# A half-rotary kernel: one DMA queue for loads and stores, six resident tiles, tables loaded by GpSimd, and whole-tile VectorE operations with the sin products in PSUM

## Chip, cores and metric

The kernel runs on one core of one Trainium2 chip. The metric is device time in microseconds (us), median over executions; the profile's "span" is 1.7 to 1.8 us shorter than the time, in runs 5 to 8 and 12 it is 1.9 to 2.2 us shorter, so differences of 0.3 us between groups of runs are not read here. All runs told of here were fast (granted clock 1.0).

The names: VectorE (DVE in the profile) does the arithmetic; SP, ACT (ScalarE) and GpSimd (POOL) here issue transfers. Each has its own DMA queue (q1 is SP's, q10 ACT's, q0 GpSimd's), and all queues feed the same 16 DMA engines. A queue that hands out its transfers in order is also called a ring. HBM is the chip's main memory; SBUF and PSUM are the core's own memories, 128 partitions each.

## The reference

`x` is 16 x 512 x 16 x 64 (batch, sequence, heads, dim) in float32, 33.55 MB; `cos` and `sin` are 512 x 32. Of each 64 elements the first 32 are rotated in two quarters of 16, and the last 32 pass through.

```python
x1, x2 = x[..., :32], x[..., 32:]
first  = x1[..., :16] * cos[..., :16] - x1[..., 16:] * sin[..., :16]
second = x1[..., :16] * sin[..., :16] + x1[..., 16:] * cos[..., :16]
return np.concatenate([first, second, x2], axis=-1)
```

All of `x` is read and all of the output is written: 67.1 MB through the core's DMA engines, with little arithmetic.

## The kernel before

A tile is 4 MB: 128 partitions with eight rows (32 KB, contiguous in HBM) each. There are T = 8 tiles. Loads go out on SP's queue, stores on ACT's; VectorE works on half tiles.

```python
K = 8; T = B * S // (P * K)                                       # T = 8 tiles
x_pool = ctx.enter_context(tc.tile_pool(name="xp", bufs=5))       # five resident tiles
ab_pool = ctx.enter_context(tc.tile_pool(name="abp", bufs=1))
stage = const_pool.tile([PB, 2, K, HF], fp32)
nc.scalar.dma_start(out=stage[:, 0]..., in_=cosf)                 # tables, ACT's queue
nc.scalar.dma_start(out=stage[:, 1]..., in_=sinf)
# ... table: four VectorE copies of stage ...
KC = 4
for t in range(T):
    x_t = x_pool.tile([P, K, H, D], fp32)
    nc.sync.dma_start(out=x_t..., in_=xf[t])                      # load, SP's queue
    for k0 in range(0, K, KC):                                    # two halves
        x1 = x_t[:, k0 : k0 + KC, :, 0:HF]
        # ... c, s: broadcast views of the table ...
        nc.vector.tensor_mul(out=a_t[:], in0=x1, in1=c)
        nc.vector.tensor_mul(out=b_t[:], in0=x1, in1=s)
        nc.vector.tensor_sub(out=x1[:, :, :, 0:Q], in0=a_t[:, :, :, 0:Q], in1=b_t[:, :, :, Q:HF])
        nc.vector.tensor_add(out=x1[:, :, :, Q:HF], in0=a_t[:, :, :, Q:HF], in1=b_t[:, :, :, 0:Q])
    nc.scalar.dma_start(out=of[t], in_=x_t...)                    # store, ACT's queue
```

Below, L0 to L7 are the loads and S0 to S7 the stores of the eight tiles.

Of the kernel before, what the change touches and what calls it, by code (L numbers as in the profile page):

```python
# [1 line left out]

# [4 lines left out]


@with_exitstack
def kernel(  # L10
    ctx: ExitStack,
    tc: tile.TileContext,
    x: bass.AP,
    cos: bass.AP,
    sin: bass.AP,
    out: bass.AP,
):
    nc = tc.nc
    fp32 = mybir.dt.float32
    P = 128  # L20
    B, S, H, D = x.shape
    Q = D // 4
    HF = D // 2


    K = 8
    T = B * S // (P * K)
    PB = S // K
    REP = P // PB

    xf = x.rearrange("b s h d -> (b s h d)").rearrange("(t p f) -> t p f", t=T, p=P)
    of = out.rearrange("b s h d -> (b s h d)").rearrange("(t p f) -> t p f", t=T, p=P)
    cosf = cos.rearrange("(p k) j -> p (k j)", k=K)
    sinf = sin.rearrange("(p k) j -> p (k j)", k=K)

    const_pool = ctx.enter_context(tc.tile_pool(name="const", bufs=1))
    x_pool = ctx.enter_context(tc.tile_pool(name="xp", bufs=5))
    ab_pool = ctx.enter_context(tc.tile_pool(name="abp", bufs=1))

    stage = const_pool.tile([PB, 2, K, HF], fp32)  # L40
    nc.scalar.dma_start(out=stage[:, 0].rearrange("p k j -> p (k j)"), in_=cosf)  # L41
    nc.scalar.dma_start(out=stage[:, 1].rearrange("p k j -> p (k j)"), in_=sinf)


    table = const_pool.tile([P, 2, K, 2, Q], fp32)
    for r in range(REP):
        for t in range(2):
            nc.vector.tensor_copy(  # L48
                out=table[r * PB : (r + 1) * PB, t],
                in_=stage[:, t, :, 0:Q].unsqueeze(2).to_broadcast((PB, K, 2, Q)),  # L50
            )
    C = table[:, 0].rearrange("p k c j -> p k (c j)")
    Sn = table[:, 1].rearrange("p k c j -> p k (c j)")

    KC = 4
    for t in range(T):
        x_t = x_pool.tile([P, K, H, D], fp32)
        nc.sync.dma_start(out=x_t.rearrange("p k h d -> p (k h d)"), in_=xf[t])  # L58
        for k0 in range(0, K, KC):
            x1 = x_t[:, k0 : k0 + KC, :, 0:HF]  # L60
            c = C[:, k0 : k0 + KC].unsqueeze(2).to_broadcast((P, KC, H, HF))
            s = Sn[:, k0 : k0 + KC].unsqueeze(2).to_broadcast((P, KC, H, HF))
            a_t = ab_pool.tile([P, KC, H, HF], fp32)
            b_t = ab_pool.tile([P, KC, H, HF], fp32)
            nc.vector.tensor_mul(out=a_t[:], in0=x1, in1=c)  # L65
            nc.vector.tensor_mul(out=b_t[:], in0=x1, in1=s)  # L66
            nc.vector.tensor_sub(  # L67
                out=x1[:, :, :, 0:Q], in0=a_t[:, :, :, 0:Q], in1=b_t[:, :, :, Q:HF]
            )
            nc.vector.tensor_add(  # L70
                out=x1[:, :, :, Q:HF], in0=a_t[:, :, :, Q:HF], in1=b_t[:, :, :, 0:Q]
            )
        nc.scalar.dma_start(out=of[t], in_=x_t.rearrange("p k h d -> p (k h d)"))


# [1 line left out]
_INS = ['x', 'cos', 'sin']  # L77
_OUTS = [((16, 512, 16, 64), 'float32')]


# [23 lines left out]
```

## Time and profile before

| | before |
|---|---|
| time, median of 3 (range) | 162.49 us (162.41 to 162.59) |
| span of the profiled run | 160.4 us |
| VectorE busy | 110.8 us (69%) |
| DMA queues, share of 16 engines | 49.3% + 48.7% |
| one 32 KB packet, median | 1.213 us |
| last VectorE instruction ends | 142.1 us |

The page of the kernel before. First busy time by engine, then the span in 40 slices of 4 us (a digit is the busy share in tenths), then the DMA queues (packets, MB, share of the 16 engines' span), the chain that ended last by line, and the VectorE groups (busy us, mean ns; after the bar, idle time before them and what ended it).

```profile
span 160.4 us, 155 instructions
...
DVE 110.8 (69%) x68; POOL 0.2 (0%) x4
...
DVE  0001599999999999999998799609995099940000
...
DMA  7999999999999999999999999999999999999993
...
DMA packets 2465, 67.25 MB, mean 419 GB/s; under 512 B 288, under 2 KB 416, under 8 KB 416
...
q1 hardware_dynamic: 1152, 33.55, 49.3%
q10 hardware_dynamic: 1312, 33.69, 48.7%
...
DMA x_t<-in_x_dram 21%; DMA out_dram<-x_t 21%; DVE b_t L66 11%; DMA stage<-in_sin_dram 10%; DVE a_t L65 10%; DVE x_t L70 5%; DVE x_t L67 4%; DVEq L99 1%; ACTq L41 0%; DVE table L48 0%; SPq L58 0%; DVEq L65 0%
...
L65 DVE TENSOR_TENSOR a_t<-x_t,table 128x2048 f32<-128x2048 f32 x16 | 36.7, 2292 | 13.6 <-DMA x_t<-in_x_dram 13.2
L66 DVE TENSOR_TENSOR b_t<-x_t,table 128x2048 f32<-128x2048 f32 x16 | 36.5, 2284 | 0.0
L67 DVE TENSOR_TENSOR x_t<-a_t,b_t 128x1024 f32<-128x1024 f32 x16 | 19.6, 1226 | 0.6
```

Read the DMA row first: it has a 9 in 38 slices, and two queues that add up to 98% of all that 16 engines can be busy. The first slice and the last are the start and the end. VectorE has holes, DMA has none. The chain of waits nevertheless gives 30% of the span to VectorE: it follows one thread of who released whom, and does not ask whether the DMA engines had other work meanwhile.

The stretches of the end before: window, its length, VectorE busy, GpSimd busy, PEclk (no matrix work here), DMA share, GB/s. A packet is counted where it starts, so short windows go above or below 1, and the last row of a run looks emptier than it was.

```profile
137.00:142.00 5.00, 4.97 (x4) 0.00 (x0) 1.00 0.99 426
142.00:157.00 15.00, 0.11 (x1) 0.00 (x0) 1.00 0.98 422
157.00:160.40 3.40, 0.00 (x0) 0.00 (x0) 1.00 0.36 154
```

VectorE is done at 142 us, and the DMA engines still have 17 us of packets queued.

### The profile page before, as it was taken

Reading aid. Unit: us, or ns where it says so; the run is one execution under the profiler, and the core shown is the slowest. Engines: PE = TensorE matmul, PEld = TensorE weight load, DVE = VectorE, ACT = ScalarE, POOL = GpSimd, SP = SyncE. Lnnn points to the kernel's source line nnn. Section 1 sums busy time; section 2 is a strip of 40 time slices with the busy share of each in tenths; the row PEclk is TensorE's granted clock in tenths of the full one; section 3 lists DMA queues with packets and bytes.
Section 4 is the critical chain, followed back from the end, with each engine's and each line's share of the span. In section 5 each row is a group of like instructions: output and inputs, shape, how many; then the busy total and the mean of one; then the engine's idle time right before and its main releaser. Section 6 shows DMA issues by size and latency. Waiting matters only on the chain.

```text
span 160.4 us, 155 instructions
## 1 busy us (share of the span) xinstructions
DVE 110.8 (69%) x68; POOL 0.2 (0%) x4
## 2 busy tenths in 40 slices
DVE  0001599999999999999998799609995099940000
POOL 0000000000000000000000000000000000000000
DMA  7999999999999999999999999999999999999993
GB/s 253 408 400 408 392 417 490 400 408 498 400 400 474 433 392 457 457 392 449 466 392 417 490 400 408 498 400 400 476 425 400 466 441 400 449 457 400 417 482 147
DMA packets 2465, 67.25 MB, mean 419 GB/s; under 512 B 288, under 2 KB 416, under 8 KB 416
## 3 DMA queue, kind: packets, MB, share of 16 engines
q1 hardware_dynamic: 1152, 33.55, 49.3%
q10 hardware_dynamic: 1312, 33.69, 48.7%
q14 instruction: 1, 0.01, 0.0%
HBM read 33.69 MB, written 33.55 MB: 419 GB/s over the span
## 4 chain that ended last, share of the span: by engine, by line
DMA 53%; DVE 30%; issue 4%; DVEq 1%; ACTq 0%; SPq 0%
DMA x_t<-in_x_dram 21%; DMA out_dram<-x_t 21%; DVE b_t L66 11%; DMA stage<-in_sin_dram 10%; DVE a_t L65 10%; DVE x_t L70 5%; DVE x_t L67 4%; DVEq L99 1%; ACTq L41 0%; DVE table L48 0%; SPq L58 0%; DVEq L65 0%
## 5 line engine op out<-in xcount | busy, mean ns | idle before, releaser
L65 DVE TENSOR_TENSOR a_t<-x_t,table 128x2048 f32<-128x2048 f32 x16 | 36.7, 2292 | 13.6 <-DMA x_t<-in_x_dram 13.2
L66 DVE TENSOR_TENSOR b_t<-x_t,table 128x2048 f32<-128x2048 f32 x16 | 36.5, 2284 | 0.0
L67 DVE TENSOR_TENSOR x_t<-a_t,b_t 128x1024 f32<-128x1024 f32 x16 | 19.6, 1226 | 0.6
L70 DVE TENSOR_TENSOR x_t<-a_t,b_t 128x1024 f32<-128x1024 f32 x16 | 19.5, 1218 | 0.0
L48 DVE COPY table<-stage 64x256 f32<-64x256 f32 x4 | 1.1, 287 | 17.1 <-DMA stage<-in_cos_dram 12.2
L88 POOL MEMSET const-bfloat16-1.0<- 128x1 bf16 x1 | 0.1, 102 | 0.0
L88 POOL MEMSET const-uint8-127<- 128x1 uint8 x1 | 0.1, 102 | 0.0
L88 POOL MEMSET const-float32-0.0<- 128x1 f32 x1 | 0.1, 99 | 0.2 <-issue 0.2
L88 POOL MEMSET const-float32-1.0<- 128x1 f32 x1 | 0.1, 99 | 0.0
## 6 DMA issues: line engine op xcount, KB each, us to landing
x_t<-in_x_dram SPq DMA_DIRECT2D x8, 4096.0 KB, 33.9
out_dram<-x_t ACTq DMA_DIRECT2D x8, 4096.0 KB, 31.3
stage<-in_cos_dram ACTq DMA_DIRECT2D x1, 64.0 KB, 11.4
stage<-in_sin_dram ACTq DMA_DIRECT2D x1, 64.0 KB, 16.3
```

The source lines that it names most:

```text
L48: nc.vector.tensor_copy(out=table[r * PB : (r + 1) * PB, t], in_=stage[:, t, :, 0:Q].unsqueeze(2).to_broadcast((PB, K, 2, Q)),)
L65: nc.vector.tensor_mul(out=a_t[:], in0=x1, in1=c)
L66: nc.vector.tensor_mul(out=b_t[:], in0=x1, in1=s)
L67: nc.vector.tensor_sub(out=x1[:, :, :, 0:Q], in0=a_t[:, :, :, 0:Q], in1=b_t[:, :, :, Q:HF])
L70: nc.vector.tensor_add(out=x1[:, :, :, Q:HF], in0=a_t[:, :, :, Q:HF], in1=b_t[:, :, :, 0:Q])
L88: nc = _bacc.Bacc("TRN2", target_bir_lowering=False, num_devices=1)
L99: with _tile.TileContext(nc) as tc:
```

## The change

It puts loads and stores on SP's queue, issues six loads ahead and each later load behind a store, loads the tables by GpSimd, and doubles the size of the VectorE operations, with the cos product in place and the sin product in PSUM (16 KB per partition), so that SBUF no longer holds the two product tiles of 8 KB per partition.

```diff
+    NB = 6
-    x_pool = ctx.enter_context(tc.tile_pool(name="xp", bufs=5))
-    ab_pool = ctx.enter_context(tc.tile_pool(name="abp", bufs=1))
+    x_pool = ctx.enter_context(tc.tile_pool(name="xp", bufs=NB))
+    b_pool = ctx.enter_context(tc.tile_pool(name="bp", bufs=1, space=bass.MemoryType.PSUM))
-    nc.scalar.dma_start(out=stage[:, 0]..., in_=cosf)      # the same for sin
+    nc.gpsimd.dma_start(out=stage[:, 0]..., in_=cosf)
-    KC = 4
+    KC = 8
+    for t in range(NB):
+        load(t)                                            # nc.sync.dma_start, as before
     for t in range(T):
-            nc.vector.tensor_mul(out=a_t[:], in0=x1, in1=c)
             nc.vector.tensor_mul(out=b_t[:], in0=x1, in1=s)
+            nc.vector.tensor_mul(out=x1, in0=x1, in1=c)
             # sub and add: a_t becomes x1
-        nc.scalar.dma_start(out=of[t], in_=x_t...)
+        nc.sync.dma_start(out=of[t], in_=x_t...)
+        if t >= 1 and t - 1 + NB < T:
+            load(t - 1 + NB)
```

(Shortened; the indices and views left out do not change.)

More of the change, by code (lines that the diff above doesn't have):

```diff
@@ L36 @@
     const_pool = ctx.enter_context(tc.tile_pool(name="const", bufs=1))
-    x_pool = ctx.enter_context(tc.tile_pool(name="xp", bufs=5))
-    ab_pool = ctx.enter_context(tc.tile_pool(name="abp", bufs=1))
+    x_pool = ctx.enter_context(tc.tile_pool(name="xp", bufs=NB))
+    b_pool = ctx.enter_context(tc.tile_pool(name="bp", bufs=1, space=bass.MemoryType.PSUM))
     stage = const_pool.tile([PB, 2, K, HF], fp32)
-    nc.scalar.dma_start(out=stage[:, 0].rearrange("p k j -> p (k j)"), in_=cosf)
-    nc.scalar.dma_start(out=stage[:, 1].rearrange("p k j -> p (k j)"), in_=sinf)
+    nc.gpsimd.dma_start(out=stage[:, 0].rearrange("p k j -> p (k j)"), in_=cosf)
+    nc.gpsimd.dma_start(out=stage[:, 1].rearrange("p k j -> p (k j)"), in_=sinf)
     table = const_pool.tile([P, 2, K, 2, Q], fp32)
@@ L53, with load @@
     Sn = table[:, 1].rearrange("p k c j -> p k (c j)")
-    KC = 4
+    KC = 8
+    tiles = []
+    def load(t):
+        x_t = x_pool.tile([P, K, H, D], fp32, name="x_t")
+        nc.sync.dma_start(out=x_t.rearrange("p k h d -> p (k h d)"), in_=xf[t])
+        tiles.append(x_t)
+    for t in range(NB):
+        load(t)
     for t in range(T):
-        x_t = x_pool.tile([P, K, H, D], fp32)
-        nc.sync.dma_start(out=x_t.rearrange("p k h d -> p (k h d)"), in_=xf[t])
+        x_t = tiles[t]
         for k0 in range(0, K, KC):
@@ L62 @@
             s = Sn[:, k0 : k0 + KC].unsqueeze(2).to_broadcast((P, KC, H, HF))
-            a_t = ab_pool.tile([P, KC, H, HF], fp32)
-            b_t = ab_pool.tile([P, KC, H, HF], fp32)
-            nc.vector.tensor_mul(out=a_t[:], in0=x1, in1=c)
+            b_t = b_pool.tile([P, KC, H, HF], fp32)
             nc.vector.tensor_mul(out=b_t[:], in0=x1, in1=s)
+            nc.vector.tensor_mul(out=x1, in0=x1, in1=c)
             nc.vector.tensor_sub(
-                out=x1[:, :, :, 0:Q], in0=a_t[:, :, :, 0:Q], in1=b_t[:, :, :, Q:HF]
+                out=x1[:, :, :, 0:Q], in0=x1[:, :, :, 0:Q], in1=b_t[:, :, :, Q:HF]
             )
             nc.vector.tensor_add(
-                out=x1[:, :, :, Q:HF], in0=a_t[:, :, :, Q:HF], in1=b_t[:, :, :, 0:Q]
+                out=x1[:, :, :, Q:HF], in0=x1[:, :, :, Q:HF], in1=b_t[:, :, :, 0:Q]
             )
-        nc.scalar.dma_start(out=of[t], in_=x_t.rearrange("p k h d -> p (k h d)"))
+        nc.sync.dma_start(out=of[t], in_=x_t.rearrange("p k h d -> p (k h d)"))
+        if t >= 1 and t - 1 + NB < T:
+            load(t - 1 + NB)
 _INS = ['x', 'cos', 'sin']
```

## The prediction

> **What bounds the kernel now.** The DMA engines, by their packets, not VectorE. The page's slices show DMA at 9 tenths or more in 38 of 40 slices; its list of queues puts 49.3% + 48.7% = 98% of the 16 engines' span on two queues. The packet records give one 32 KB packet 1.213 us (median) in either direction, alone or interleaved. Work: 16 transfers of 128 packets are 128 packets per engine, 128 x 1.213 = 155.3 us. The first packet starts at 1.7 us, the last ends at 159.2, the span ends at 160.4. So only 159.2 - 1.7 - 155.3 = 2.2 us are not the floor: the first sixteen packets take up to 2.1 us each, the tables' 1 KB packets cost some tenths, and engines finish unevenly. The Trainium skill ("DMA: Bandwidth & Descriptors", Where 436 GB/s comes from) gives a fabric ceiling of 435 GB/s; the trace agrees: 16 x 32,768 B in 1.213 us is 432 GB/s.
>
> VectorE is busy 110.8 us (69%). Its waits (13.2 us for x, 17.1 us for the tables) lie under full DMA queues. The chain of waits names VectorE for 30%, but the DMA engines never ran dry meanwhile.
>
> **What the change does.**
> - One queue: the same page (Issuing engines are not separate DMA queues) says all DMAs run on the same 16 engines, and the trace agrees: packets of the loads-only start, the mixed middle and the stores-only end all take 1.213 us, and the single-queue phases keep share 1.0 across DMA boundaries. Gain: 0.
> - Order becomes L0-L5, S0, S1, L6, S2, L7, S3-S7. Estimate at 9.7 us per transfer: loads end at 60 us; S0 by 70; L6 goes at about 72, while S1 has 8 us queued; L7 at about 82 behind L6 and S2. Tile t is computed about 18 + 13.4(t+1) us: S0 ready at 31 (needed at 60), S7 at about 125 (needed at 147). The ring should not run dry.
> - VectorE: an estimate from 2.29 us (2048 elements) and 1.22 us (1024) is 0.157 us + 1.07 us per 1024: 4.42 us and 2.29 us for the doubled sizes. Per tile 13.8 falls to about 13.3-13.6 us, busy total about 108 us. PSUM operands may return some. Off the critical path: 0.
> - Tables by GpSimd: landing 12.2 and 16.3 us may move a few us; slack before the first store is about 28 us: 0, save a few tenths for start or end of GpSimd's DMA.
>
> **Prediction.** The gain stays off the critical path: 162.3 us, within 161.2 to 164.0 (8 in 10). Faster by over 2%: 2%; within 2%: 95%; slower by over 2%: 3%.
>
> **What would show it.** One queue's share becomes about 98%; 32 KB packets stay at 1.21 us; 9s in the slices from 2 to 157 us. VectorE's waits for x fall from 13.2 to under 4 us, and its last instruction ends near 125 us instead of 142, with no gain in time; its four operations become about 4.4, 4.4, 2.3 and 2.3 us. The gap from VectorE's end to the span's end grows from 18 to about 33 us, all DMA.
>
> **What would make it wrong.** A hole in the ring: SP blocked on a semaphore while its ring empties (DMA share under 0.9 near 60-90 or 130-147 us), at most a few us; a GpSimd set-up at start or end of over 3 us; packets that in one ring take more than 1.21 us. Faster by 2% would need packets under 1.19 us, which nothing here suggests.

## The result, and the profile after

The changed kernel takes 162.34 us (median of 6, 162.21 to 162.44) against 162.45 us for the kernel before in the same rounds. The ratio is 0.9992, with a 95% interval of 0.998 to 1.0005: no change. Here and below a ratio is the mean time of one kernel's fast runs over that of the other's in the same rounds, so it is not quite the ratio of the medians quoted.

The page after, the same lines:

```profile
span 160.6 us, 118 instructions
...
DVE 107.9 (67%) x36; POOL 1.4 (1%) x6
...
DVE  0025999999999999999999999982999000000000
...
DMA  7999999999999999999999999999999999999994
...
DMA packets 2368, 67.24 MB, mean 419 GB/s; under 512 B 288, under 2 KB 288, under 8 KB 320
...
q1 hardware_dynamic: 2304, 67.11, 97.8%
q0 software_dynamic: 64, 0.13, 0.2%
...
DMA x_t<-in_x_dram 26%; DMA out_dram<-x_t 26%; DVE b_t L73 8%; DVE x_t L74 8%; DVE x_t L78 3%; DVE x_t L75 2%; DVEq L109 1%; DVEq L73 0%
...
L73 DVE TENSOR_TENSOR b_t<-x_t,table 128x4096 f32<-128x4096 f32 x8 | 35.5, 4432 | 5.7 <-DMA x_t<-in_x_dram 5.5
L74 DVE TENSOR_TENSOR x_t<-x_t,table 128x4096 f32<-128x4096 f32 x8 | 35.4, 4424 | 0.3
L75 DVE TENSOR_TENSOR x_t<-x_t,b_t 128x2048 f32<-128x2048 f32 x8 | 18.3, 2286 | 0.3
```

And its end:

```profile
120.00:125.00 5.00, 4.70 (x3) 0.00 (x0) 1.00 1.02 439
125.00:157.00 32.00, 0.00 (x0) 0.00 (x0) 1.00 1.00 432
157.00:160.60 3.60, 0.00 (x0) 0.00 (x0) 1.00 0.34 146
```

One queue now has the 98% that two had, and the DMA row has not moved. VectorE did become better: it starts tiles at 13.7 us instead of 18.3 us, needs 13.45 us per tile instead of 13.85 us, waits 5.5 us for x instead of 13.2 us, and is through at 124.7 us instead of 142.1 us. The tail of nothing but stores, at 432 GB/s, grew by the same 17 us. (Run 2 will show that the early end comes from the order of the single ring, and not from the faster operations.)

How the single ring is issued, from the timeline after (start, duration of the issue with waits inside a group):

```profile
0.74 3.02 SPq L61 DMA_DIRECT2D x_t<-in_x_dram  x6
...
27.14 13.79 SPq L81 DMA_DIRECT2D out_dram<-x_t  x2
...
72.16 0.34 SPq L61 DMA_DIRECT2D x_t<-in_x_dram  x1
...
82.22 0.34 SPq L61 DMA_DIRECT2D x_t<-in_x_dram  x1
...
82.65 42.44 SPq L81 DMA_DIRECT2D out_dram<-x_t  x5
```

L6 goes out at 72.16 us, when S0 has landed, and at that time S1 is still in the ring. So the ring does not run dry while SP waits.

The tables landed sooner, 7.2 and 9.3 us after issue instead of 11.4 and 16.3. Here the profile and the Trainium skill read well together: "DMA: Bandwidth & Descriptors" (Queues, rings and completion order) says that a DMA engine takes turns between its rings packet by packet. The packet counts above show that ACT's queue moved the tables in 128 packets of 1 KB (416 - 288), and GpSimd's in 32 of 4 KB (320 - 288). That is eight against two per engine. In the trace before, the table packets start in rounds 1.25 us apart, so each stands behind a 1.2 us packet of x, and fewer packets land sooner. The trace agrees with the page; VectorE starts earlier by it, but the time gains nothing (run 11).

### The profile page after: what moved, and what is told of

Same layout as the page of the kernel before. It is cut to its first block, busy times and chain, and to the rows that moved or that the text cites. A ratio compares the mean times of both kernels' runs of the same rounds, so it can differ in the third digit from the quotient of the medians.

```text
span 160.6 us, 118 instructions
## 1 busy us (share of the span) xinstructions
DVE 107.9 (67%) x36; POOL 1.4 (1%) x6
## 4 chain that ended last, share of the span: by engine, by line
DMA 52%; DVE 21%; issue 3%; DVEq 1%
DMA x_t<-in_x_dram 26%; DMA out_dram<-x_t 26%; DVE b_t L73 8%; DVE x_t L74 8%; DVE x_t L78 3%; DVE x_t L75 2%; DVEq L109 1%; DVEq L73 0%
## 5 line engine op out<-in xcount | busy, mean ns | idle before, releaser
L73 DVE TENSOR_TENSOR b_t<-x_t,table 128x4096 f32<-128x4096 f32 x8 | 35.5, 4432 | 5.7 <-DMA x_t<-in_x_dram 5.5
L74 DVE TENSOR_TENSOR x_t<-x_t,table 128x4096 f32<-128x4096 f32 x8 | 35.4, 4424 | 0.3
L75 DVE TENSOR_TENSOR x_t<-x_t,b_t 128x2048 f32<-128x2048 f32 x8 | 18.3, 2286 | 0.3
L78 DVE TENSOR_TENSOR x_t<-x_t,b_t 128x2048 f32<-128x2048 f32 x8 | 18.2, 2279 | 0.0
L42 POOL DMA_DIRECT2D stage<-in_cos_dram x1 | 0.6, 648 | 0.8 <-PEq L109 0.8
L43 POOL DMA_DIRECT2D stage<-in_sin_dram x1 | 0.5, 518 | 0.0
```

Source lines behind the costliest of these rows:

```text
L42: nc.gpsimd.dma_start(out=stage[:, 0].rearrange("p k j -> p (k j)"), in_=cosf)
L43: nc.gpsimd.dma_start(out=stage[:, 1].rearrange("p k j -> p (k j)"), in_=sinf)
L74: nc.vector.tensor_mul(out=x1, in0=x1, in1=c)
L75: nc.vector.tensor_sub(out=x1[:, :, :, 0:Q], in0=x1[:, :, :, 0:Q], in1=b_t[:, :, :, Q:HF])
L78: nc.vector.tensor_add(out=x1[:, :, :, Q:HF], in0=x1[:, :, :, Q:HF], in1=b_t[:, :, :, 0:Q])
```

## The experiments

The theory: the kernel's time is the packets of 16 transfers on 16 engines, 128 x 1.213 = 155.3 us, plus some 7 us of start and end; everything else is worth nothing unless it lets the engines run dry. The first rival: the change had a real gain (VectorE) and a real loss (the single queue) that cancelled. The second: VectorE lies on the path, as the chain of waits draws it. Twelve kernels were run; all results were correct except that of the first. The kernel before took 162.44 to 162.49 us (medians) beside them.

### 1. No VectorE work at all

```diff
-        for k0 in range(0, K, KC):
-            ...                      # all four operations
```

> The changed kernel with all four VectorE operations of every tile taken away (output wrong on purpose: it is a copy of x). Theory (the 16 transfers alone make the time; VectorE lies wholly behind them): no change, 162.3 us (161.8 to 162.7), span near 160.6 us, the 32 KB packets at 1.21 us, DMA slices full from 2 to 157 us. Rival (VectorE and its hand-overs, 21% of the chain of waits, still hold part of the time): 3 us or more faster.

Measured: 162.04 us, ratio to before 0.9973 (0.996 to 0.9985). The page of this run:

```profile
DVE 1.1 (1%) x4; POOL 1.4 (1%) x6
...
DMA  7999999999999999999999999999999999999994
```

Taking away 107 us of VectorE work leaves 99.8% of the changed kernel's time. The second rival falls: VectorE's share of the chain was 21%, and its share of the time is at most about 0.3 us (162.34 - 162.04, in other rounds, and the two intervals overlap).

### 2. The stores back on ACT's queue

```diff
-        nc.sync.dma_start(out=of[t], in_=x_t...)
+        nc.scalar.dma_start(out=of[t], in_=x_t...)
```

> The changed kernel with the stores back on ACT's queue (two queues, everything else changed). Theory (which queue carries a packet costs nothing as long as neither queue's emptiness leaves the engines idle): 162.3 us, within 0.4%; the two queues share about 98% again and the packets keep 1.21 us. Rival (a gain of the VectorE part and a loss of the single queue cancel in the change): 1% or more faster than the changed kernel.

Measured: 161.76 us, ratio 0.9961 (0.9948 to 0.9974). The change in the time is 0.4% against before, and its interval lies below that of the changed kernel (0.998 to 1.0005), measured in other rounds. So the first rival is wrong at the size that it named (1%), and right at a smaller one: the single queue does cost about half a microsecond. Run 12 returns to it.

This run also shows what the single queue is good for. VectorE has the same operations as in the changed kernel (107.9 us), but it waits 26.6 us for x instead of 5.5 us and is through at 146.1 us instead of 124.7 us: with two queues the stores share the DMA engines with the later loads, while the single ring finishes six loads first.

### 3. The VectorE part alone

```diff
-    KC = 4
+    KC = 8
-            nc.vector.tensor_mul(out=a_t[:], in0=x1, in1=c)
             nc.vector.tensor_mul(out=b_t[:], in0=x1, in1=s)      # b_t in PSUM
+            nc.vector.tensor_mul(out=x1, in0=x1, in1=c)
```

> The kernel before with only the VectorE part of the change (whole tile, in place, sin products in PSUM), two queues, five tiles, tables by ACT. Theory: 162.4 us, within 0.4% of before, although VectorE's work per tile falls from 13.85 to 13.45 us and its last instruction ends 2 to 4 us earlier. Rival (gain of VectorE cancelled elsewhere): 1 to 3 us faster than before.

Measured: 163.44 us (162.46 to 163.94), ratio 1.0054 (1.0029 to 1.008). VectorE's work shrank as expected, to 107.9 us, and there is no gain; but 1 us of loss was not expected. Nor was VectorE's end: it was to come 2 to 4 us earlier and came at 144.0 us, 1.9 us later than before, since VectorE waited 18.3 us for x instead of 13.2 us. To see where it is, I followed the trace's packet records end to start; they fall into 16 unbroken chains of 128 packets of 32 KB, one for each DMA engine. Fifteen engines end between 158.1 and 158.6 us, and one ends at 160.4 us. It has no gap: its packets after 20 us took 1.6 us more in total than 1.213 us each, those of the others less than 0.15 us. The span ends 1.2 us after that last engine, as it does before and after. Why that one engine was slower in this kernel is not settled; the kernel before has a milder case, one packet of 1.8 us at 112.6 us on the engine that ends last, at 159.2 us.

### 4. The queue part alone

```diff
-        nc.scalar.dma_start(out=of[t], in_=x_t...)
+        nc.sync.dma_start(out=of[t], in_=x_t...)    # nothing else; kernel before
```

> The kernel before with only its stores moved to SP's queue, without the loads issued ahead and without the later load placement. The scheduler then issues L0-L2, S0-S2, L3-L5, S3-S5, L6, L7, S6, S7 on the one queue, so loads stand behind stores that wait for VectorE. Theory (one queue costs nothing of itself, but a store that waits for compute holds back the loads behind it and the ring empties): holes of about 4 us each before S1, S2, S5, S7 and 6 us before S6, in all about 23 us: 185 us (178 to 192), with the packets still at 1.21 us. Rival (order of issue is of no weight, since the DMA engines have the same bytes to move): 162 to 165 us.

Measured: 185.23 us, ratio 1.1401. The holes are where the timetable put them, before S1, S2, S5, S6 and S7:

```profile
42.00:46.00 4.00, 3.93 (x4) 0.00 (x0) 1.00 0.31 131
55.00:59.00 4.00, 3.44 (x3) 0.00 (x0) 1.00 0.00 0
118.00:123.00 5.00, 3.94 (x3) 0.00 (x0) 1.00 0.42 177
151.00:158.00 7.00, 6.93 (x5) 0.00 (x0) 1.00 0.19 80
168.00:172.00 4.00, 3.55 (x3) 0.00 (x0) 1.00 0.00 0
```

In each of these stretches VectorE is busy and the DMA share is low or zero: a store waits for its tile, and the loads behind it wait with it. The single queue is harmless in the change only because the change also sets the order of issue.

The holes are not quite all of the 23 us, and the expectation that packets stay at 1.21 us missed in part (the median is still 1.213 us). The mean engine has 159.5 us of 32 KB packets, 2.9 us more than before. The slow ones stand where the ring turns, in either direction: from S2 to L3 (16 packets at 68 us, 1.6 to 2.4 us each), from L5 to S3 (26 from 96.4 to 98.5 us) and from S5 to L6 (16 at 131.4 us).

### 5 and 6. Three and four resident tiles

```diff
-    NB = 6
+    NB = 3      # run 5;  NB = 4 in run 6
```

> The changed kernel with three resident tiles instead of six. Theory (the ring's timetable with 9.7 us per transfer, about 1.3 us to landing, 13.45 us of VectorE per tile): L7 can only be issued after S4 has landed, lands near 140 us, its tile is computed by 154 us, while S6 is through at about 149 us; the ring is dry for about 6 us before S7: 168.4 us (166 to 171). Rival (resident tiles do not matter, or they matter smoothly with every tile less): 162.3 us, or a hole spread over the whole run.

Measured: 171.33 us, ratio 1.0551 (1.0534 to 1.0569). The hole before S7 is there, but the sum is 3 us over the expected 168.4 and just outside the range. Stretches of this run, a slow one early with the one before it, and the hole before S7:

```profile
46.00:50.00 4.00, 3.96 (x2) 0.00 (x0) 1.00 1.12 483
50.00:54.00 4.00, 4.00 (x2) 0.00 (x0) 1.00 0.89 303
...
152.00:158.00 6.00, 4.89 (x3) 0.00 (x0) 1.00 0.20 87
```

S7 is issued at 156.9 us, where 154 was expected. The timetable is late from its first turn from a store to a load: S0 ended near 42 us, so that S1, L3 (9.7 us each) and 1.3 us to landing should have let VectorE start on L3 at 62.7 us, and it started at 65.2. Around 50.8 us, where S1 ends and L3 begins, sixteen packets took 1.5 to 2.1 us instead of 1.213 us, and one at 52.8 us took 2.4 us; the stretch from 50 to 54 us moves 303 GB/s instead of about 430 (part of this is the counting of packets where they start: the stretch before has 483). Where L3 ends and S2 begins, at 60 to 61.3 us, sixteen packets again took 1.7 to 2.3 us. The mean engine has 158.5 us of 32 KB packets in this run and 156.8 in the changed kernel. The step that failed in my expectation was the constant 9.7 us per transfer.

> The changed kernel with four resident tiles instead of six. Theory (same timetable): S7 is computed at about 143 us and needed at about 149 us, no hole anywhere: 162.3 us within 0.4%, though VectorE waits for x much more than with six tiles (20 us or more against 5.5 us). Rival (each resident tile taken away costs): slower by 1% or more.

Measured: 163.22 us, and a spread that no other run has, 162.36 to 164.74; ratio 1.0062 (1.0024 to 1.0099). The forecast of 162.3 us within 0.4% missed. The profile is of the slowest of the six executions (164.74 us). There is no hole in the middle, but there is an end that the theory did not have:

```profile
152.00:158.00 6.00, 0.00 (x0) 0.00 (x0) 1.00 1.01 437
158.00:160.00 2.00, 0.00 (x0) 0.00 (x0) 1.00 0.16 66
160.00:162.00 2.00, 0.00 (x0) 0.00 (x0) 1.00 0.04 16
```

Four packets start between 158 and 160 us (66 GB/s for 2 us is 132 KB) and one after 160. By the chains, fourteen engines end by 159.3 us and two at 160.7 and 161.5 us. The slow packets of this run, summed over the engines by transfer:

```
last one or two packets of   L4 (70 us)  L5 (90 us)  L6 (110 us)  L7 (128 us)
us over 1.213 each             1.42        0.71         1.13         4.47
```

They stand last in a load that has a store behind it in the ring. The changed kernel has the same thing at L5 to S0 (4.1 us over all engines), L6 to S2 (2.5) and L7 to S3 (0.4), but spread more evenly, so that its last engine ends at 159.34 us. The run with the stores on ACT's queue (run 2) has three packets over 1.3 us at 30 us, just before its first store begins, none later, and its engines end between 158.38 and 158.74 us.

### 7, 8 and 9. More VectorE work: after, after, and before

```diff
             nc.vector.tensor_mul(out=b_t[:], in0=x1, in1=s)
+            nc.vector.tensor_mul(out=b_t[:], in0=x1, in1=s)      # 8: after; 9: before
+            # 7: after, on the first half of b_t, x1 and s only
```

> The changed kernel with half of the sin product of each tile computed twice (same result): VectorE works about 2.25 us more per tile, 18 us in all. Theory: tile 7 is ready near 139 us and S7 is needed near 149 us, so no change: 162.3 us within 0.4%. Rival (VectorE is on the path, as the chain of waits draws it): slower by 3 us or more.

> The changed kernel with the whole sin product of each tile computed twice (same result): VectorE works about 4.47 us more per tile, 36 us in all. Theory: tile 7 is ready near 157 us, the ring is dry for about 9 us before S7: 171.5 us (169.5 to 173), so 36 us of work cost about 9. Rival (VectorE lies on the path throughout): near 198 us.

> The kernel before with the sin product of every half tile computed twice (same result): about 4.5 us more VectorE work per tile, as in the changed kernel's run with the whole product doubled. Theory (the change bought slack, not time): compute starts at 18.3 us instead of 13.7 and takes 18.4 us a tile, tile 7 is ready near 165.5 us: about 179 us (177 to 182), 8 us worse than the changed kernel with the same extra product. Rival (the change bought no slack either): the same time as that run, about 171.5 us.

| run | VectorE busy | time | ratio to before |
|---|---|---|---|
| 1: changed kernel, no work | 1.1 us | 162.04 us | 0.9973 |
| changed kernel | 107.9 us | 162.34 us | 0.9992 |
| 7: with half a product more | 126.3 us | 162.29 us | 0.9994 |
| 8: with a whole product more | 143.3 us | 171.31 us | 1.0548 |
| 9: before, with a whole product more | 147.5 us | 179.89 us | 1.1069 |

From 1 to 126 us of VectorE work the time does not move by more than 0.3 us. At 143 us it has passed the edge. The stretches of run 8:

```profile
144.00:149.00 5.00, 4.96 (x2) 0.00 (x0) 1.00 0.99 426
149.00:158.00 9.00, 8.20 (x3) 0.00 (x0) 1.00 0.00 0
158.00:169.00 11.00, 0.00 (x0) 0.00 (x0) 1.00 0.89 381
```

No packet starts between 149 and 158 us; by the packet records the engines stand still from 150 to 158 us, until the last tile is computed (157.2 us), and for under 1 us before S6. The run is 9 us longer. In the kernel before the same extra product costs 17.4 us (179.89 - 162.49). So the change did buy something, which this kernel does not need: slack. Before, VectorE ended 17 us ahead of the last packet, of which S7's own transfer takes 9.7; after, 35 us ahead. The kept traces tell which part bought it: with the same VectorE operations, but without the single queue, VectorE ends at 146.1 us (run 2), and the VectorE part alone ends at 144.0 us (run 3), both later than the kernel before. The tables on ACT's queue cost about 1 us of it (run 11 ends at 125.6 us). The single ring with four tiles (run 6) does not have it either: 146.3 us. So the slack comes from the order of the single ring together with the six tiles, which let six loads go first.

### 10. Packets of 4 KB instead of 32 KB

```diff
-    xf = x.rearrange("b s h d -> (b s h d)").rearrange("(t p f) -> t p f", t=T, p=P)
+    xf = x.rearrange("b s h d -> (b s) (h d)").rearrange("(t k p) f -> t p k f", t=T, p=P)
+    # of likewise; the tables arranged to match
```

> The changed kernel with a tile's rows dealt to the partitions so that each contiguous piece in HBM is one row of 4 KB instead of eight rows of 32 KB (same bytes, same number of transfers, same VectorE work, right result). Theory (the floor is the engines' packet time, which fits 8.4 ns + bytes/27.2 per ns: 9 ns for 4 B, 46 ns for 1 KB, 159.5 ns for the tables' 4 KB and 1213 ns for 32 KB in the records): 1024 packets per engine per direction pair take 163.3 us instead of 155.3: 170.3 us (168.5 to 172). Rival (the floor is bytes per second, whatever the packets): 162.3 us.

Measured: 169.39 us, ratio 1.0429 (1.0414 to 1.0444). The queue in the page of this run:

```profile
DMA packets 16704, 67.24 MB, mean 402 GB/s; under 512 B 288, under 2 KB 288, under 8 KB 16704
```

The same bytes in the same number of transfers, with the same compute, take 7 us longer. So the time goes with the packets and not with the bytes alone. The size was expected as 8 us from the fit to recorded durations (median here 159.0 ns). It is a little less, since in this run the recorded packets of an engine overlap: on average 16.4 of 16 are under way. One thing is not separated: an engine's successive pieces now also lie far apart in HBM.

### 11. The tables back on ACT's queue

```diff
-    nc.gpsimd.dma_start(out=stage[:, 0]..., in_=cosf)    # both
+    nc.scalar.dma_start(out=stage[:, 0]..., in_=cosf)
```

> The changed kernel with the two table loads back on ACT's queue. Theory: VectorE starts its first tile near 18 us instead of 13.7 us and ends some 0 to 4 us later; time unchanged, 162.3 us within 0.4%. Rival (the tables' way weighs, a gain or a loss hidden in the change): a change of 1% or more.

Measured: 162.18 us, ratio 0.9984 (0.9967 to 1.0002). VectorE gets its last table at 17.5 us again, is through at 125.6 us instead of 124.7 us, and the time is the same.

### 12. Four tiles on two queues

```diff
-    NB = 6
+    NB = 4
-        nc.sync.dma_start(out=of[t], in_=x_t...)
+        nc.scalar.dma_start(out=of[t], in_=x_t...)
```

> The changed kernel with four resident tiles and the stores on ACT's queue; it differs from the four-tile run on one queue only in the stores' queue. There 32 KB load packets that stand last before a store in the one ring were slow (5 such turns, 1.3 to 2.3 us instead of 1.21), two engines ended 1.4 and 2.2 us after the rest, and the six times spread over 162.36 to 164.74. Theory A (the turns from load to store within one ring make single engines late): with two rings no such packets, the 16 engines end within 1 us of one another, 162.0 us (161.6 to 162.6), spread under 0.6 us. Theory B (four tiles are too few, and the lateness comes from hand-overs between landing and issue): as on one queue, near 163.2 us with a wide spread, or worse, with holes in the DMA slices.

Measured: 162.01 us (161.91 to 162.20), ratio 0.9971 (0.9957 to 0.9986). (Run 6 ran on another chip; the kernel before took 162.44 us beside run 6 and 162.48 us beside this one.) The end of this run, beside that of run 6 above:

```profile
152.00:158.00 6.00, 0.00 (x0) 0.00 (x0) 1.00 1.01 437
158.00:160.00 2.00, 0.00 (x0) 0.00 (x0) 1.00 0.00 0
```

No packet starts after 158 us, where run 6 had five. By the chains the 16 engines end within 0.3 us, from 158.39 to 158.70 us. With everything else as in run 6, moving the stores to another ring took away the late engines, the slow last packets of the loads after 31 us (ten at 30 us remain), and the spread. Theory A's forecast is met and B's is not; four tiles are enough. That one ring or two decides is shown; that the turn itself is the cause is not, for moving the stores also changes how loads and stores interleave. It is not the turn alone: runs 1, 7 and 8 have the changed kernel's order on the same ring, with 1, 126 and 143 us of VectorE work, and after 20 us they have one, five and four packets over 1.3 us, where the changed kernel has 31. So neither the order nor the amount of VectorE work decides it alone (one profiled execution of each).

No version beats both kernels by anything that matters. The best is run 2, 161.76 us, 0.4% below the kernel before.

## Why the prediction was right

- **The bound.** "The DMA engines, by their packets, not VectorE" held: no VectorE work at all gives 162.04 us (run 1), 18 us more gives 162.29 us (run 7), and changing only the packets gives 169.39 us (run 10).
- **The sum.** 162.3 us was predicted and 162.34 measured. That it fits to 0.04 us is luck (see the last point); that it fits to 1 us is not. First packet at 1.75 us, 155.3 us of packets, last packet at 159.3 us, span 160.6 us.
- **The order of the ring.** L6 was expected "at about 72" and went at 72.2 us, L7 at about 82 and went at 82.2, S7's tile at about 125 and was ready at 124.7. That the ring would not run dry was the condition on which it all hung; runs 4, 5 and 8 break it in three ways and lose 23, 9 and 9 us.
- **VectorE.** Expected 4.4, 4.4, 2.3 and 2.3 us, 108 us busy; measured 4.43, 4.42, 2.29 and 2.28 us, 107.9 us. The Trainium skill ("VectorE: DVE Perf Modes", The TRN2 errata) gives (N + 151)/0.96 ns for a float32 `tensor_tensor` add, measured there up to N = 2048. As an estimate that is 4424 ns for N = 4096, and the trace has 4424 and 4432 for the products.
- **A detail that missed.** VectorE's wait for x was to be under 4 us and was 5.5 us: the tables came so early that it now waited 1.9 us for L0 too, beside 3.5 us for L7.
- **A step that was too simple.** "Gain: 0" for the single queue rested on phases of the trace before in which a ring carries loads only or stores only. That trace has no turn from load to store within one ring, so it could not show what such turns do. Run 2 puts the cost of the single queue at about 0.5 us here, and runs 6 and 12 at 1.2 us with four tiles. How much of it the slow packets at the turns make is not shown: run 7 has almost none and takes 162.29 us (span 160.3 us), run 2 161.76 us (160.0 us), the changed kernel 162.34 us (160.6 us), so by the times they make next to nothing of it and by the spans half. The part of GpSimd (run 11) is within the noise. So there was a small loss in the change, and something small that balances it; what that is I cannot name, since the VectorE part alone (run 3) came out 0.5% slower.

## What to carry to other kernels

If the DMA queues' shares add up to 98% and a packet's duration times the packets per engine gives the span, then arithmetic, buffers, and the choice of queue can gain only the few microseconds at the ends, whatever the chain of waits says, though a bad order can still lose much (run 4); look for fewer bytes, and do not cut the packets small (run 10; packets over 32 KB were not tried). In these runs a single queue for loads and stores was safe only where at every wait of the issuing engine there was more queued work than the wait was long: draw the timetable of the ring first. Where time does not move, ask for slack: adding work to both kernels showed in two runs what the change had bought, and an experiment that takes one part away (run 2) shows which part bought it.

## What the Trainium skill lacked or had wrong

- "DMA: Bandwidth & Descriptors", Issuing engines are not separate DMA queues: it says that issuing from several engines only saves issue time. The runs show a second effect: in one ring, packets at a turn between loads and stores took up to 2.4 us instead of 1.213 us (runs 4, 5 and 6, but hardly any in runs 1, 7 and 8), and with four tiles one ring took 163.22 us (162.36 to 164.74) and two rings 162.01 us (161.91 to 162.20).
- The same page, Specifications, has 512 B and more as enough for line rate, though the page elsewhere counts a fixed overhead for every packet: pieces of 4 KB instead of 32 KB cost 4.3% here (169.39 us against 162.49 for the kernel before), with the more scattered HBM order of run 10 not separated from it.
- The same page, Latency and other measured facts, knows two engines that are usually slower and, as a guess, suspects GpSimd's descriptor rings. Run 3 has no DMA of GpSimd at all, and still one engine ends 1.8 us behind the other fifteen; in run 6 it is two, 1.4 and 2.2 us behind the next. (The records here do not name the engines.) What makes an engine late on SP's and ACT's queues is on no page that I found.
- "VectorE: DVE Perf Modes", The TRN2 errata: its table gives 62 cycles more for PSUM to SBUF than for SBUF to SBUF. In this `tensor_tensor` with one of its two inputs in PSUM nothing of that shows: 2286 ns for 2048 elements, against 2284 to 2292 ns with all operands in SBUF.
